# Layer 1's embedding products moved from the first layer's last attention head to the point between the last gate product and the latent attention

## The chip, the cores and the metric

The kernel runs on one core of one Trainium2 chip. The metric is the device time of one execution in microseconds (us), the median of several runs. Before the change it is 1482.28 us, the median of three runs from 1481.83 to 1483.80.

## What is computed

A decoder trunk of two layers on 1024 tokens of width 1024, in float32. Cut to what matters here:

```
def reference(x, p, ...):
    h = x
    for i in range(2):
        hn = rmsnorm(h, norm_g[i])
        m = even_layer(hn, ...) if i % 2 == 0 else odd_layer(hn, ...)
        h = h + m
        h = h + sigmoid(h @ ple_w_gate[i]) * (p[i] @ ple_w_proj[i])
    return h

def odd_layer(h, ...):
    z = h @ w_in
    cq, ckv, k_rope, c_gate, qkv, d_b, d_a, d_gate = split(z)
    # latent attention, 4 heads of 128: causal softmax(q k^T / sqrt(192)) v, gated by silu(c_gate)
    # gated delta rule, 4 heads of 128, chunks: one triangular solve a chunk, then a scan; gated by silu(d_gate)
    return concatenate([oc, od]) @ w_out
```

The even layer (layer 0) has a pooling mixer and six heads of differential attention. The products `p[i] @ ple_w_proj[i]`, 1024 x 256 by 256 x 1024, are the "embedding products": they depend on the inputs alone, and may be done at any time before the last step of their layer.

## The kernel before

**Products.** Each float32 operand is split into a rounded high part and the rest (`split`: a cast on ScalarE, line 134, and a difference on VectorE, line 135), and each product is three matmuls, high x high, high x low and low x high (lines 142 to 144). A bank of 128 x 512 results with a depth of 256 is thus six matmuls. One layer's embedding products are 8 output blocks (j in two groups of four) x 2 halves of the tokens = 16 banks = 96 matmuls.

**Order.** The program is written as Python generators that are stepped side by side; a list scheduler then sets each engine's order, and each engine runs its list strictly in that order. Accumulator banks in PSUM are shared: two called `acc`, two `s`, one `tr`, one `o`, two `x`. Loads and stores are nearly all issued by SyncE (SP) in one list; a store that has to wait for its data holds back all that stands behind it in that list.

**Layer 0's last part.** Heads 0 to 4 of the differential attention have the next head's projection beside them as filling work. Head 5 has no next head, so `ple_both()` fills it: the embedding products of layer 0 and of layer 1, one after the other. The results are copied from PSUM to tiles `z` (ScalarE line 127, VectorE line 129, in turn) and stored to `ple` in HBM. What of it is not used up beside head 5 is done after it. Then `out_stage` multiplies the mixer's output by `w_out`.

**Layer 1's middle.** After the projections come two products for the gates (`gate_proj`, here `gp1` is the second one, token tiles t0 to t7, 24 matmuls each; lines 907 to 909). Beside it stand the last preparation of the delta rule (`gdn_prep`), `block_solve` (the inverse of all 32 x 32 triangular blocks, 62 VectorE instructions that follow each from the one before, lines 990 and 992, whose result `xinv` goes to HBM and comes back as `U`), and `mla_prep` of head 0: for each half of the tokens it loads `zk`, `zq` and `V`, and transposes 4 x 4 blocks (line 1138) into one `acc` bank at a time, from which ScalarE (line 1139) and VectorE (line 1140) make the high and low parts of K and Q. The tags `zq` have two buffers, one for zk and one for zq, so the second half can be loaded only when the first half's transposes have read theirs. After this the latent attention (`mla_attn`: scores lines 1155 to 1159, softmax line 257, transposes line 275, values line 268) runs beside the delta rule (`gdn_solve`, from line 1000; `gdn_half`).

```
block_solve(nt)
istack.close()
istack, mp = open_pool("mla")
...
ahead = mla_prep(0, st)
step(ahead, gp1, gp1, ahead, ahead, gp1, gp1, ahead, gp1)
```

The functions that the change touches:

Of the kernel before, what the change touches and what calls it, by code (L numbers as in the profile page):

```python
# [56 lines left out]
def trunk_kernel(ctx, tc, a, out, layers=2):  # L57
# [520 lines left out]
        finish(1)  # L578
        yield

    def ple_both():

        for layer in range(layers):
            slots = [xt() for _ in range(8)]
            pT = [[None, None] for _ in range(2)]
            for h in range(2):
                for k in range(2):
                    hi, lo = slots[4 * h + 2 * k], slots[4 * h + 2 * k + 1]
                    split(hi, lo, stage(a["pT"][layer, k * P:(k + 1) * P, h * 512:(h + 1) * 512]))
                    pT[k][h] = (hi, lo)  # L590
            for gq in range(2):
                if gq == 0:
                    yield
                w = wload(a["ple_w_proj"][layer], 512 * gq, 512, nk=2)
                for j in range(4):
                    t = T("z", 2, (2, 512))
                    for h in range(2):
                        ps = bank("acc")
                        proj_T(pT, w, j, h, ps)
                        copy(h, t[:, h], ps)  # L600
                        dma.dma_start(ple[layer][4 * gq + j][h], t[:, h])
                    yield

    def fresh():
        return dict(Q=[], K=[], V=[], G=[])
# [13 lines left out]
    for hd in range(6):  # L619
        at, late = even_attn(hd, st), ahead  # L620
        if hd < 5:
            st = fresh()
            ahead = even_proj(hd + 1, st)
        else:
            ahead = ple_both()
        step(at, at, ahead, late, done, at, at, ahead, at, at, ahead, at, ahead, at, at)
        done = at
    step(done)
# [491 lines left out]
            s.activation(ct, tr, AF.Identity, scale=onorm)  # L1120
            dma.dma_start(cat[1][4 + hd][h], ct)

    def mla_prep(hd, st):
        for h in range(2):
            zq, zk = T("zq", 2, (4, 256), pool=mp), T("zq", 2, (4, 256), pool=mp)

            Q, K, V = T("Q", 3, (3, 512), F32R, mp), T("K", 3, (4, 512), F32R, mp), T("V", 4, pool=mp)
            for n, t in (("Q", Q), ("K", K), ("V", V)):
                st[n].append(t)
            dma.dma_start(zk, qkv[h][:, :, hd, 256:512])  # L1130
            dma.dma_start(zq, qkv[h][:, :, hd, 0:256])
            dma.dma_start(c3(V), qkv[h][:, :, hd, 512:640])
            yield
            for z, lo, dst, hb, lb, part in ((zk, 0, K, 2, 3, slice(0, P)), (zk, P, K, 0, 1, slice(0, P)),
                                             (zq, 0, Q, 1, 2, slice(0, P)), (zq, P, Q, 0, 0, slice(64, P))):
                ps = bank("acc")
                for c in range(4):
                    pe.transpose(ps[:, c * P:(c + 1) * P], z[:, c, lo:lo + P], ident)  # L1138
                s.copy(dst[:, hb, :], ps)
                v.tensor_tensor(out=dst[part, lb, :], in0=ps[part], in1=dst[part, hb, :].bitcast(F32), op=ALU.subtract)  # L1140
            yield
# [73 lines left out]
            step(cv, prep, cv, prep, cv, prep, prep)  # L1215
            prep = gdn_prep(hd, h, *outs)
    step(gp1, prep, gp1, prep, gp1, prep, prep)
    block_solve(nt)
    istack.close()
    istack, mp = open_pool("mla")  # L1220
    PW[0], PBUFS[1] = T_, 1
    PBUFS[0] = 2
    st = dict(Q=[], K=[], V=[])
    ahead = mla_prep(0, st)
    step(ahead, gp1, gp1, ahead, ahead, gp1, gp1, ahead, gp1)
    bstack.close()
    xstack.close()
    sstack, pools["scan"] = open_pool("scan", "right")
    astack, pools["y"] = open_pool("attn")

    def gdn():
        parts = [(pair, h, {}) for pair in ((0, 1), (2, 3)) for h in range(2)]
# [7 lines left out]
        sstack.close()  # L1240

    rec = gdn()
    for hd in range(H):
        at = mla_attn(hd, st)
        st = dict(Q=[], K=[], V=[])
# [80 lines left out]
```

## Time and profile before

| | |
|---|---|
| median of three runs | 1482.28 us |
| profiled execution | 1483.52 us |
| its span, first to last instruction | 1481.8 us |
| mean granted TensorE clock | 0.990 of full speed |
| TensorE (PE) busy | 1420.4 us, 96% of the span |
| VectorE (DVE) busy | 988.9 us, 67% |
| ScalarE (ACT) busy | 662.1 us, 45% |
| GpSimd (POOL) busy | 212.6 us, 14% |
| HBM read and written | 161 MB, 109 GB/s over the span |

The profile is of one execution. "Idle before" in its rows is the time that an engine stood still before an instruction, with the instruction of another engine that ended the wait. PEld is the loading of weights into TensorE, beside its matmuls. The granted clock has two levels, 2.4 GHz (1.0) and 1.2 GHz (0.5); a window's value between them is a mean over it. Matmuls are pipelined, so their durations overlap: what a matmul takes in a stream is the distance between two starts. An engine's busy share is a mean over stages with different limits.

### The profile page before, as it was taken

Reading aid. Unit: us, or ns where it says so; the run is one execution under the profiler, and the core shown is the slowest. Engines: PE = TensorE matmul, PEld = TensorE weight load, DVE = VectorE, ACT = ScalarE, POOL = GpSimd, SP = SyncE. Lnnn points to the kernel's source line nnn. Section 1 sums busy time; section 2 is a strip of 40 time slices with the busy share of each in tenths; the row PEclk is TensorE's granted clock in tenths of the full one; section 3 lists DMA queues with packets and bytes.
Section 4 is the critical chain, followed back from the end, with each engine's and each line's share of the span. In section 5 each row is a group of like instructions: output and inputs, shape, how many; then the busy total and the mean of one; then the engine's idle time right before and its main releaser. Section 6 shows DMA issues by size and latency. Waiting matters only on the chain. (4 is left out here: it accounts for less than half of the span.)

```text
span 1481.8 us, 22778 instructions
## 1 busy us (share of the span) xinstructions
PE 1420.4 (96%) x7495; PEld 1157.4 (78%) x7495; DVE 988.9 (67%) x2926; ACT 662.1 (45%) x1652; POOL 212.6 (14%) x347
## 2 busy tenths in 40 slices
PE   8899999999998999999998999999889999999998
PEld 6677888888887778888886777888768888877886
DVE  8645767676676857356668789988577888643342
ACT  6325656565656742134445434443223446722220
POOL 6230101011111001012104441110000000000021
PEclk9899999999999999999999999999989999999999
DMA  6215323232335582344424343233455634343432
GB/s 215 61 49 131 86 72 99 59 107 51 100 94 156 157 275 76 95 132 144 119 49 141 152 148 116 94 122 130 141 178 177 219 120 148 122 149 100 128 107 85
DMA packets 127749, 181.52 MB, mean 123 GB/s; under 512 B 28536, under 2 KB 55440, under 8 KB 127632
## 3 DMA queue, kind: packets, MB, share of 16 engines
q1 hardware_dynamic: 127632, 180.08, 39.8%
q8 instruction: 59, 0.97, 0.3%
q14 instruction: 58, 0.48, 0.1%
HBM read 108.20 MB, written 52.95 MB: 109 GB/s over the span
## 5 line engine op out<-in xcount | busy, mean ns | idle before, releaser
L142 PE MATMUL acc<-wh,x 128*128 128x512 f32 (+1 forms) x576 | 230.6, 401 | 0.6 <-DVE g L465 0.4
L143 PE MATMUL acc<-wl,x 128*128 128x512 f32 (+1 forms) x576 | 228.9, 397 | 1.7 <-DVE wl L135 1.7
L144 PE MATMUL acc<-wh,x 128*128 128x512 f32 (+1 forms) x576 | 227.3, 395 | 0.0
L142 PE MATMUL acc<-x,wh 128*128 128x512 f32 x536 | 215.8, 403 | 4.5 <-ACT wh L134 3.2
L144 PE MATMUL acc<-x,wl 128*128 128x512 f32 x536 | 214.0, 400 | 4.0 <-DVE wl L135 4.0
L143 PE MATMUL acc<-x,wh 128*128 128x512 f32 x536 | 212.5, 397 | 0.0
L134 ACT CAST wh<-raw 128x512 fp32r<-128x512 f32 (+2 forms) x184 | 106.8, 600 | 81.2 <-PE acc L143 37.5
L135 DVE TENSOR_TENSOR wl<-raw,wh 128x512 fp32r<-128x512 f32 (+2 forms) x184 | 120.7, 674 | 28.9 <-ACT wh L134 27.2
L143 PEld LDWEIGHTS acc<-wl,x 128*128 128x128 f32 x576 | 108.7, 189 | 25.3 <-DVE wl L135 2.8
L142 PEld LDWEIGHTS acc<-wh,x 128*128 128x128 f32 x576 | 108.5, 189 | 24.2 <-PE acc L144 0.8
L144 PEld LDWEIGHTS acc<-wh,x 128*128 128x128 f32 x576 | 108.5, 188 | 22.5
L144 PEld LDWEIGHTS acc<-x,wl 128*128 128x128 f32 x536 | 101.3, 189 | 30.4 <-DVE wl L135 7.1
L142 PEld LDWEIGHTS acc<-x,wh 128*128 128x128 f32 x536 | 101.0, 189 | 29.5 <-ACT wh L134 4.0
L143 PEld LDWEIGHTS acc<-x,wh 128*128 128x128 f32 x536 | 101.2, 189 | 22.4 <-issue 0.2
L680 POOL TENSOR_TENSOR u<-hp,hp 128x512 f32<-128x512 f32 x32 | 44.3, 1385 | 486.9 <-DVE hp L135 206.6
L261 ACT ACTIVATE p<-p,mx 128x128 f32<-128x128 f32 (+7 forms) x128 | 99.4, 777 | 32.9 <-DVE mx L257 24.1
L143 PE MATMUL acc<-hp,wh 128*128 128x512 f32 x256 | 101.6, 397 | 0.0
L142 PE MATMUL acc<-hp,wh 128*128 128x512 f32 x256 | 101.5, 396 | 0.0
L144 PE MATMUL acc<-hp,wl 128*128 128x512 f32 x256 | 101.5, 396 | 0.0
L257 DVE CUSTOM_DVE_ANT_0 p<-s,cst 128x512 f32<-128x512 f32 (+3 forms) x128 | 74.1, 585 | 29.4 <-PE s L534 15.4
L678 DVE SCALAR_TENSOR_TENSOR th<-th,ld 128x512 f32<-128x512 f32 x32 | 27.1, 848 | 77.2 <-ACT th L676 75.4
L461 ACT ACTIVATE z<-acc,rstd 128x256 f32<-128x256 f32 x48 | 22.8, 475 | 102.2 <-PE acc L144 99.4
(466 smaller groups left out, 2855.5 us busy)
## 6 DMA issues: line engine op xcount, KB each, us to landing
raw<-in_ev_w_in SPq DMA_DIRECT2D x56, 256.0 KB
Q<-sq SPq DMA_DIRECT2D x96, 128.0 KB
qkv<-zz SPq DMA_DIRECT2D x16, 640.0 KB
raw<-cat SPq DMA_DIRECT2D x32, 256.0 KB
ple<-z SPq DMA_DIRECT2D x32, 256.0 KB
raw<-in_ple_w_gate SPq DMA_DIRECT2D x32, 256.0 KB
ld<-ple SPq DMA_DIRECT2D x32, 256.0 KB
zq<-qkv SPq DMA_DIRECT2D x16, 512.0 KB
```

The source lines that it names most:

```text
L134: s.copy(hi, src)
L135: v.tensor_tensor(out=lo, in0=src, in1=hi.bitcast(F32), op=ALU.subtract)
L142: pe.matmul(ps, lh, rh, start=first, stop=False)
L143: pe.matmul(ps, lh, rl, start=False, stop=False)
L144: pe.matmul(ps, ll, rh, start=False, stop=last)
L257: v.tensor_tensor_reduce(out=pm[:, c * 512:c * 512 + n], in0=ps[:, 0:n], in1=mk, scale=-scale, scalar=prev, op0=ALU.add, op1=ALU.min, accu ...
L261: s.activation(pm[:, 0:w], pm[:, 0:w], AF.Exp, bias=prev, scale=-1.0, accum_out=sums)
L461: s.activation(z[:, t % 4, :], ps[:, 0:256], AF.Identity, scale=rstd[0][:, t:t + 1])
L678: v.scalar_tensor_tensor(out=th, in0=th, scalar=1.0, in1=r, op0=ALU.add, op1=ALU.mult)
L680: g.tensor_tensor(out=u, in0=hi.bitcast(F32), in1=lo.bitcast(F32), op=ALU.add)
```

## The change

`ple_both()` becomes `ple_proj(layer, slot, outs)`. Layer 0's embedding products stay beside head 5; each result is now a `z` tile of its own (two buffers, where two results shared a tile before). Layer 1's are started (loads and splits of `p`) in a new pool behind the opening of the pool `mla`; their 16 banks are stepped after the last gate tile and before the pool of the latent attention is opened. Their results go to the tiles `raw` (four buffers), the tag of the weights' loads, all copied by ScalarE. `block_solve` is written behind the opening of the pool and behind the first step of the embedding products. The first `mla_prep` takes its banks in turn from `s` and `x` (two each) in place of `acc`, and is stepped in turn with the gate tiles in another pattern.

```diff
-    def ple_both():
...
+    def ple_proj(layer, slot, outs):
+
+        pT = [[None, None] for _ in range(2)]
+        for h in range(2):
+            for k in range(2):
+                hi, lo = slot(), slot()
+                split(hi, lo, stage(a["pT"][layer, k * P:(k + 1) * P, h * 512:(h + 1) * 512]))
+                pT[k][h] = (hi, lo)
+        yield
+        for gq in range(2):
+            w = wload(a["ple_w_proj"][layer], 512 * gq, 512, nk=2)
+            for j in range(4):
+                for h in range(2):
+                    ps, t = bank("acc"), outs()
+                    proj_T(pT, w, j, h, ps)
+                    copy(h * (1 - layer), t, ps)
+                    dma.dma_start(ple[layer][4 * gq + j][h], t)
+                yield
...
-            ahead = ple_both()
+            ahead = ple_proj(0, xt, lambda: T("z", 2, (2, 512))[:, 0])
...
-    def mla_prep(hd, st):
+    def mla_prep(hd, st, banks=("acc",)):
+        nb = 0
...
-                ps = bank("acc")
+                ps = bank(banks[nb % len(banks)])
+                nb += 1
...
-    block_solve(nt)
     istack.close()
     istack, mp = open_pool("mla")
+    fstack, fp = open_pool("embed")
+    fill = ple_proj(1, lambda: T("pT", 8, dt=F32R, pool=fp), lambda: wp.tile([P, 512], F32, tag="raw", bufs=4, name=nm("ple")))
+    step(fill)
+    block_solve(nt)
...
-    ahead = mla_prep(0, st)
-    step(ahead, gp1, gp1, ahead, ahead, gp1, gp1, ahead, gp1)
+    ahead = mla_prep(0, st, ("s", "x"))
+    step(ahead, gp1, gp1, ahead, gp1, ahead, gp1, ahead, gp1)
...
-    astack, pools["y"] = open_pool("attn")
...
     rec = gdn()
+    step(*[fill] * 8)
+    fstack.close()
+    astack, pools["y"] = open_pool("attn")
```

Where instructions stand before and after, at three places. First TensorE's list at the end of head 5 before the change (`tr` are the last transposes of head 5, `acc1602` the last bank of layer 0's embedding products, `acc1622` the first bank of layer 1's):

```order
L143 MATMUL acc1602_6013<-x1422_5426,wh1589_5941 128x512
L564 MATMUL tr1580_5907<-cst_66,o1476_5584 128x128 x2
L144 MATMUL acc1602_6013<-x1421_5425,wl1590_5942 128x512
L564 MATMUL tr1580_5907<-cst_66,o1476_5584 128x128 x2
L142 MATMUL acc1622_6059<-x1603_6022,wh1616_6047 128x512
L143 MATMUL acc1622_6059<-x1604_6023,wh1616_6047 128x512
```

and the same place after the change (`acc1609` is the last bank of layer 0's embedding products, `acc1659` the first bank of `out_stage`):

```order
L564 MATMUL tr1583_5910<-cst_66,o1477_5585 128x128 x4
L142 MATMUL acc1609_6020<-x1421_5431,wh1590_5939 128x512
L143 MATMUL acc1609_6020<-x1422_5432,wh1590_5939 128x512
L144 MATMUL acc1609_6020<-x1421_5431,wl1591_5940 128x512
L142 MATMUL acc1609_6020<-x1424_5437,wh1593_5945 128x512
L143 MATMUL acc1609_6020<-x1425_5438,wh1593_5945 128x512
L144 MATMUL acc1609_6020<-x1424_5437,wl1594_5946 128x512
L142 MATMUL acc1659_6133<-x1611_6037,wh1636_6086 128x512
```

The 96 matmuls of layer 1's embedding products no longer stand between head 5 and `out_stage`. Two more banks of layer 0's stand behind the last values of head 5 than before.

Second, TensorE's list in layer 1's middle before the change, at the end of gate tile t4 (`acc2733`); `zq` are the loaded q and k tiles of head 0, the first four rows of L1138 their first half's transposes, L1155 and L1156 the first scores, and `acc2744` gate tile t5, behind which t6 and the second half's transposes follow:

```order
L144 MATMUL acc2733_11591<-wh2690_11294,x1994_7780 128x512
L1138 MATMUL acc2735_11620<-cst_66,zq2727_11555 128x128 x4
L1138 MATMUL acc2736_11627<-cst_66,zq2727_11555 128x128 x4
L1138 MATMUL acc2737_11634<-cst_66,zq2726_11554 128x128 x4
L1138 MATMUL acc2738_11641<-cst_66,zq2726_11554 128x128 x4
L1155 MATMUL s2757_11783<-K2729_11557,Q2728_11556 128x128
L1156 MATMUL s2757_11783<-K2729_11557,Q2728_11556 128x128
L1155 MATMUL s2776_11880<-K2729_11557,Q2728_11556 128x256
L1156 MATMUL s2776_11880<-K2729_11557,Q2728_11556 128x256
L142 MATMUL acc2744_11656<-wh2669_11252,x1888_7261 128x512
```

and after the change (`acc2718` is gate tile t6, which follows t5 directly; L1136 are the same transposes; `acc2724` is t7):

```order
L144 MATMUL acc2718_11520<-wh2650_11102,x1954_7588 128x512
L1136 MATMUL s2707_11455<-cst_66,zq2699_11390 128x128 x4
L1136 MATMUL x2708_11462<-cst_66,zq2699_11390 128x128 x4
L1136 MATMUL s2709_11469<-cst_66,zq2698_11389 128x128 x4
L1136 MATMUL x2710_11476<-cst_66,zq2698_11389 128x128 x4
L1136 MATMUL s2720_11549<-cst_66,zq2714_11513 128x128 x4
L1136 MATMUL x2721_11556<-cst_66,zq2714_11513 128x128 x4
L142 MATMUL acc2724_11577<-wh2629_11060,x1848_7069 128x512
L143 MATMUL acc2724_11577<-wl2630_11061,x1848_7069 128x512
```

Both halves' transposes now stand one behind the other between t6 and t7. Behind t7 the 96 matmuls of the embedding products follow, with the first two tiles of scores between their halves.

Third, VectorE's list at the end of `block_solve` before the change (`nx` is the inverse, L257 the first softmax, L1016 the transposes of `U`, which comes back from `xinv`):

```order
L990 TENSOR_TENSOR tm_11484<-nx_11483,nx_9531 128x31
L992 TENSOR_TENSOR nx_11483<-nx_11483,tm_11484 128x31
L908 SCALAR_TENSOR_TENSOR gz_11767<-gz_11767,acc_11742 128x512
L257 ISA p_11782,mx_11789<-s_11783,cst 128x128
L257 ISA mx_11789 128x1
L257 ISA p_11879,mx_11886<-s_11880,cst 128x256
```

and after the change (L986 and L988 are the solve, `wl` the low parts of the second half of the embedding weights, L1012 to L1014 the transposes of `U`):

```order
L986 TENSOR_TENSOR tm_11323<-nx_11322,nx_9339 128x31
L988 TENSOR_TENSOR nx_11322<-nx_11322,tm_11323 128x31
L135 TENSOR_TENSOR wl_11705<-raw_11703,wh_11704 128x512
L135 TENSOR_TENSOR wl_11711<-raw_11709,wh_11710 128x512
L1012 STREAM_TRANSPOSE wk_11828<-U_11817 32x32 x4
L1013 STREAM_TRANSPOSE wk_11828<-U_11817 32x32 x4
L1014 STREAM_TRANSPOSE wk_11828<-U_11817 32x32 x4
L1012 STREAM_TRANSPOSE wk_11932<-U_11921 32x32 x3
L257 ISA p_11802,mx_11809<-s_11803,cst 128x128
```

The first softmax now stands behind the transposes of `U`, and so behind the way of `xinv` to HBM and back.

And SP's list after the change, at the same place (`ple` are the stores of the embedding results, each of which waits for its copy, `U` the loads of the inverse):

```order
L158 DMA raw_11703<-in_ple_w_proj 128x512
L597 DMA ple_3_1_122<-ple_11694 128x512
L158 DMA raw_11709<-in_ple_w_proj 128x512
L989 DMA xinv<-nx_11322 128x1024
L999 DMA L_11920<-gL_0_7661 128x512
L1004 DMA vb_11928<-gvb_0_7653 128x512
L1005 DMA kw_11929<-gkw_0_7637 128x512
L1002 DMA U_11817<-xinv 32x4x32
L597 DMA ple_4_0_123<-ple_11716 128x512
L597 DMA ple_4_1_124<-ple_11726 128x512
L1002 DMA U_11817<-xinv 32x4x32
L597 DMA ple_5_0_125<-ple_11736 128x512
```

The loads of the second half of the embedding weights, the store of `xinv` and the four loads of the first `U` stand among the stores; the fourth load of `U` stands behind the fifth of the second half's eight stores.

## Rows read from the trace of the kernel before

**Rows 1.** The page's first part: busy time, share of the span, instructions.

```profile
PE 1420.4 (96%) x7495; PEld 1157.4 (78%) x7495; DVE 988.9 (67%) x2926; ACT 662.1 (45%) x1652; POOL 212.6 (14%) x347
```

**Rows 2.** Timeline of TensorE, end of head 5 (start, duration, count [idle before]).

```profile
525.03 0.48 PE L142 MATMUL acc<-x,wh 128*128 128x512 f32 x1
...
526.05 0.39 PE L143 MATMUL acc<-x,wh 128*128 128x512 f32 x1
526.28 0.40 PE L144 MATMUL acc<-x,wl 128*128 128x512 f32 x1
...
548.64 0.50 PE L142 MATMUL acc<-x,wh 128*128 128x512 f32 x1
```

**Rows 3.** Groups by line, 524 to 550 us: ScalarE's copies of embedding results.

```profile
L127 ACT COPY z<-acc 128x512 f32<-128x512 f32 x8 | 4.7, 587 | 8.6 <-DMA ple<-z 5.8 <-PE acc L144 2.6
```

**Rows 4.** Timeline of TensorE beside head 5.

```profile
479.23 1.97 PE L493 MATMUL x<-cst,z 128*128 128x128 f32 x8 [2.68 <-POOL z L242]
```

**Rows 5.** Windows: length, busy PE, PEld, DVE, ACT, POOL; PEclk, DMA, GB/s.

```profile
1060.00:1070.00 10.00, 5.72 (x28) 4.29 (x26) 4.67 (x16) 1.75 (x3) 0.00 (x0) 0.97 0.70 214
1070.00:1080.00 10.00, 9.50 (x36) 7.79 (x37) 9.14 (x22) 1.17 (x2) 0.00 (x0) 0.69 0.51 155
1080.00:1090.00 10.00, 8.88 (x48) 6.96 (x46) 8.42 (x20) 3.03 (x5) 0.00 (x0) 1.00 0.19 55
1090.00:1100.00 10.00, 7.17 (x30) 4.97 (x28) 6.80 (x22) 1.77 (x4) 1.49 (x4) 1.00 0.60 188
1100.00:1110.00 10.00, 7.36 (x60) 5.21 (x60) 5.65 (x28) 2.58 (x8) 0.00 (x0) 0.66 0.92 279
1110.00:1340.00 230.00, 223.25 (x1766) 191.42 (x1767) 163.35 (x617) 110.93 (x236) 7.94 (x14) 1.00 0.50 155
```

**Rows 6.** Timeline of TensorE in layer 1's middle.

```profile
1066.12 0.66 PE L1138 MATMUL acc<-cst,zq 128*128 128x128 f32 x4 [1.06 <-DVE gz L908]
1070.50 1.97 PE L1138 MATMUL acc<-cst,zq 128*128 128x128 f32 x8 [3.72 <-DVE K L1140]
...
1073.31 0.63 PE L142 MATMUL acc<-wh,x 128*128 128x512 f32 x1
1073.73 0.63 PE L143 MATMUL acc<-wl,x 128*128 128x512 f32 x1
...
1098.01 0.44 PE L1155 MATMUL s<-K,Q 128*128 128x384 f32 x1 [1.71 <-DVE mx L257]
...
1102.64 0.80 PE L268 MATMUL o<-V,pt 128*128 128x128 f32 x2 [3.43 <-DVE r L1163]
```

**Rows 7.** The same windows at 1 us: clock and DMA traffic.

```profile
1070.00:1071.00 1.00, 0.50 (x3) 0.50 (x4) 1.00 (x3) 0.00 (x0) 0.00 (x0) 0.50 1.09 355
1071.00:1072.00 1.00, 1.00 (x6) 0.87 (x5) 0.91 (x3) 0.35 (x1) 0.00 (x0) 0.50 0.41 126
1098.00:1099.00 1.00, 0.90 (x4) 0.55 (x4) 0.00 (x0) 0.48 (x2) 0.00 (x0) 1.00 0.99 383
```

**Rows 8.** Timeline of SP: issues of loads and stores.

```profile
1066.81 0.53 SPq L1130 DMA_DIRECT2D zq<-qkv  x1
...
1096.69 0.33 SPq L993 DMA_DIRECT2D xinv<-nx  x1
...
1099.42 0.32 SPq L1006 DMA_DIRECT2D U<-xinv  x1
```

**Rows 9.** Timeline of VectorE: block_solve's first and last, first softmax, U.

```profile
1065.98 0.18 DVE L990 TENSOR_TENSOR tm<-nx,nx 128x31 f32<-128x31 f32 x1
...
1096.42 0.21 DVE L992 TENSOR_TENSOR nx<-nx,tm 128x31 f32<-128x31 f32 x1
...
1097.66 0.28 DVE L257 CUSTOM_DVE_ANT_0 p<-s,cst 128x128 f32<-128x128 f32 x1
...
1102.75 0.48 DVE L1016 STREAM_TRANSPOSE wk<-U 32x32 f32<-32x32 f32 x4
```

**Rows 10.** Page's fifth part: splits' low part on VectorE.

```profile
L135 DVE TENSOR_TENSOR wl<-raw,wh 128x512 fp32r<-128x512 f32 (+2 forms) x184 | 120.7, 674 | 28.9 <-ACT wh L134 27.2
```

More of the change, by code (lines that the diff above doesn't have):

```diff
@@ L579, in even_attn @@
         yield
-    def ple_both():
[L583 to L597, printed above, removed]
-                        ps = bank("acc")
[L599 to L602, printed above, removed]
+    def ple_proj(layer, slot, outs):
[15 more added lines that the diff above has]
+                yield
     def fresh():
@@ L1135, in mla_prep @@
                                              (zq, 0, Q, 1, 2, slice(0, P)), (zq, P, Q, 0, 0, slice(64, P))):
-                ps = bank("acc")
+                ps = bank(banks[nb % len(banks)])
+                nb += 1
                 for c in range(4):
```

## The prediction

> **What bounds the kernel now.** I read the page's busy times first: TensorE works 1420.4 of 1481.8 us [rows 1], so a change can win only what TensorE loses in idle stretches or at the lower clock, or what it does needlessly. The work itself stays the same here: every product, transpose and solve is there before and after. So the question is in which of its holes TensorE will stand afterwards. The timeline of TensorE answers that in two stretches.
>
> The first is the end of head 5. Layer 1's embedding products follow head 5's last transposes without a wait from 525.03 to 548.64 us, 23.6 us for 96 matmuls; the starts inside are 0.233 us apart [rows 2]. They fill no hole there; they are pure TensorE time ahead of `out_stage`.
>
> The second is layer 1's middle. In the windows from 1060 to 1110 us TensorE is busy for 5.72, 9.50, 8.88, 7.17 and 7.36 of 10 us, 38.6 of 50 together, and in two of them the mean granted clock is 0.69 and 0.66 [rows 5]. From 1110 to 1340 us it is busy 223 of 230 at full clock: there is nothing to fill later. So idle time in this middle is 50 - 38.6 = 11.4 us, most of it in four waits: 1.06 and 3.72 us between the first transposes, 1.71 for the softmax of the first scores, 3.43 for the first softmax's sum [rows 6]. The clock costs on top of it. After the 3.72 us of idleness the matmuls start 0.42 us apart [rows 6], the clock is at its lower level, 1.2 GHz [rows 7]; a mean of 0.69 over the window from 1070 is 6.2 us at half speed, of which TensorE worked 5.6: 2.8 lost. After the 3.43 us it is the same from 1102.6 to about 1106.5, some 2 lost (0.66 in that window, a part of it idle).  Holes before, in us of full-speed TensorE: 11.4 + 2.8 + 2.1 = 16.3.
>
> **What the move takes away.** At the end of head 5 the 96 matmuls go. If nothing else moved, `out_stage` would start 23.6 us earlier. Two things take from that. Two more banks of layer 0's embedding products (12 matmuls, 12 x 0.233 = 2.8 us) stand behind head 5's last values than before, and the values end when head 5's softmax chain lets them, not when the products do. And beside head 5 the wait of 2.68 us for GpSimd [rows 4] has one group of transposes and fewer products ahead of it than before. Also each result now has a `z` buffer of its own, two in all, while before two results shared one of two, four in all; ScalarE's copies already waited 5.8 us for stores in this stretch [rows 3]. Halved buffering may hold up the last banks by as much as that, or by nothing since only a few banks are left back to back. I take 23.6 - 2.8 - 0.5 = 20.3 us gained, with ends at 23.6 (the two banks stand in a hole) and 17.5 (another 2.8 lost to the wait for GpSimd and the copies).
>
> **What it puts in, in the middle.** 96 matmuls at 0.233 us are 22.4 us; their 16 copies on ScalarE (0.59 us each [rows 3], 9.4 us) lie beside them, one for every 1.4 us of TensorE. Now the holes. Without the transposes between t4 and t5, t5 and t6 (48 matmuls, 11.2 us) run on from 1064.46 to 1075.7, and the first half's transposes, in four banks, no longer wait for one another: the 1.06 and 3.72 us go, and the lower clock behind them. They end at about 1077. But the second half's transposes now stand right behind, and the tags `zq` have two buffers, so `zk` of the second half is loaded only after the first half's zk transposes have read it, at about 1076.4. In the trace that load was issued at 1066.81 [rows 8]; it and a load behind it, 0.77 MB, move until 1071.4 at about 355 GB/s [rows 7], so its own 512 KB took some 3.8 us. Hence 1080.2, and a wait of **3.2 us** in the place of 3.72. As 3.72 us of idleness brought the lower clock, I count its 2.8 us once more. t7 then ends at about 1080.2 + 5.6 + 1.6 for the transposes + 2.8 = 1090.2.
>
> The first half of the products takes 11.2 us, to 1101.4, the first two tiles' scores 1.3. The second half's weights come late. Their loads stand in SP's list behind the stores of the seventh and the eighth result, and these tiles and the weights share the four buffers of `raw`. So the loads issue only at about 1101 and 1102.5. Nothing in the trace shows this load in this place; with the 3.8 us of zk as an upper end and the 2.73 us from the store of xinv to the first load of `U` [rows 8] as a lower one, they land from 1104 to 1106, and cast and low part (0.59 and 0.67 us [rows 3, 10]) come on top. That is a hole of **3.4 us** (between 1 and 5, and up to 2.8 more if the clock falls again). Holes after: 3.2 + 2.8 + 3.4 = 9.4.
>
> `block_solve` runs on VectorE from 1065.98 to 1096.42 with K's and Q's low parts in between [rows 9]. It starts as before, but the first low part of K stands after its 13th instruction and waits for the transposes behind t6: VectorE stands for some 6 us, and the embedding weights' low parts (0.67 us each) join. So it ends at about 1104, not 1096.4. Behind it stands xinv's way out and back, 6.3 us from 1096.42 to the first transpose of `U` at 1102.75 [rows 9]. The first softmax, before at 1097.66 [rows 9], now stands behind these transposes, at 1111 to 1117. The second half of the products covers TensorE until 1105.5 + 11.2 = 1116.7: the cover is just long enough. From there on the stretch is dense as before.
>
> **The sum.** The middle comes out later against its start by 22.4 + 9.4 - 16.3 = 15.5 us; the end of head 5 gives 20.3. Net 15.5 - 20.3 = -4.8 us. The profiled execution took 1483.5 and the median is 1482.3, so the forecast is 1478.7 against the one and **1477.5** for the median.
>
> **A rule against it.** The row first: after 3.72 us of idleness the clock was at its lower level, and after the 1.71 us before 1098.01 it was not (1.00 in the window of 1098) [rows 6, 7]. The Trainium skill ("TensorE: Matmul & The Clock Gate", part 1) says that the throttled clock is the default and that only activity releases it, so that each wait is paid again after it ends. By that, the third wait would bring 2.8 us more, and the sum would be -2.0 instead of -4.8; by the row of 1.71 us alone it would not. This trace shows the clock falling after the long waits and not after the short ones, and a wait of 3.4 us is nearer to the long ones; it stands in the range.
>
> **Rivals.**
> *Larger gain.* The holes are small: the second half's zk comes before its transposes are reached, the weights' loads are issued early. Then about 2.9 us of holes are left, the middle costs 22.4 + 2.9 - 16.3 = 9.0, the end of head 5 gives the full 23.6: -14.6, **1467.7**. For it: before, transposes of the same kind followed with waits of 0.2 to 0.5 us once the data lay there. Against: two buffers for `zq`.
> *No change.* All three waits take their upper ends, with the clock: holes of 3.2 + 2.8 + 5 + 2.8 = 13.8, the middle costs 19.9: **1482**. For it: SP's list, and DMA traffic of 279 GB/s over the window from 1100 with 383 at its height [rows 5, 7], to which 4 MB of stores come (16 x 256 KB), now in that stretch.
> *Slower.* The solve becomes the bound. The loads of `U` stand between the stores of the second half's results; a store that waits for its copy holds `U` back, and behind `U` stand the transposes, and behind them the first softmax. If the last needed `U` goes out only behind the last copies (1116.7 + 0.6), it lands 2.7 us later at 1120; the transposes take 1.5, the softmax to the first values 5 (1097.66 to 1102.64): 1126.5 against 1102.64, 23.9 later, less 2.7 of scores done ahead: 21.2. With 17.5 gained at head 5 that is +3.7, **1486**. It decides from the point where the middle is later by more than the 17.5 to 20.3 gained. For it: the first softmax's new place in VectorE's list. Against: four loads of `U` are enough for the first transposes, and the fourth stands behind the fifth of eight stores only.
> In a sentence by itself: the Trainium skill ("DMA: Bandwidth & Descriptors", on the anatomy of one DMA) says that waits happen on the issuing sequencer before dispatch, which is this mechanism, and that one transfer has a fixed cost of about 2.0 us; by its figures the first `U` load would land 2.0 us after its issue, and the slower case would be 1485. No row shows a `U` load held by a store.
>
> **Chances.** Forecast 0.42, larger gain 0.24, no change 0.20, slower 0.14. A measurement of this kernel can tell 0.2%, 3 us, from no change. The forecast's own range is 1473 to 1481; the part of it within the bound and the part of the no-change case below it are about equal, so faster is 0.66, same 0.20, slower 0.14. The range for 8 in 10 leaves out the far ends: 1467.5 to 1484.
>
> **What would show it.** Right: `out_stage` begins near 528 us; no idleness between t4 and t6, one wait of about 3 us before the second half's transposes with the lower clock after it; a second wait before the second half of the products; first softmax between 1091 and 1097 on the new clock (the old less 20). Wrong: `out_stage` begins after 532, TensorE waits for head 5's copies, a wait stands behind the products for the first softmax, or the attention after it loses its 97% density.

## The result and the profile after

The changed kernel takes 1478.91 us (median of 18 runs, 1476.07 to 1481.43), the kernel before 1485.93 in the same comparison (18 runs, 1481.83 to 1492.26). The ratio is 0.9945, with a 95% interval from 0.9932 to 0.9959: faster by 0.55%, some 8 us by the ratio and 7.0 by the medians. Forecast were 1477.5 us, faster, against a median of 1482.3 from three runs. The two profiled executions lie closer together, 1483.52 and 1479.85, 3.7 us apart; why that is less than the medians' 7.0 is settled further down. In the experiments below, two runs of the banks alone (1709 and 2782 us) and two of the kernel before (2775 and 3530) are left out of the ratios.

The first part of the page after answers to [rows 1]: the same 7495 matmuls, TensorE's busy time within 1.4 us of before, in a span that is 3.9 us shorter (1477.9).

```profile
PE 1419.0 (96%) x7495; PEld 1158.4 (78%) x7495; DVE 985.1 (67%) x2918; ACT 666.2 (45%) x1660; POOL 207.0 (14%) x347
```

The end of head 5, in TensorE's timeline after (start, duration, count, idle before in brackets), answers to [rows 2, 4]:

```profile
477.43 0.33 PE L493 MATMUL x<-cst,z 128*128 128x128 f32 x1 [1.72 <-POOL z L242]
...
525.09 1.02 PE L564 MATMUL tr<-cst,o 128*128 128x128 f32 x4 [1.01 <-DVE o L557]
526.07 0.50 PE L142 MATMUL acc<-x,wh 128*128 128x512 f32 x1
...
527.58 0.40 PE L142 MATMUL acc<-x,wh 128*128 128x512 f32 x1
```

Behind head 5's transposes stands one bank of layer 0's products (526.07), and at 527.58 `out_stage` begins, before at 548.64. The wait for GpSimd has become shorter, 1.72 instead of 2.68 us, and the lower clock that stood behind it before (0.50 from 479 to 482 us, some 1.5 us lost) is gone.

Layer 1's middle, in TensorE's timeline after, answers to [rows 6]:

```profile
1062.90 1.08 PE L1136 MATMUL s<-cst,zq 128*128 128x128 f32 x4 [3.11 <-DMA zq<-qkv]
...
1071.65 0.39 PE L142 MATMUL acc<-pT,wh 128*128 128x512 f32 x1
...
1083.25 0.22 PE L1154 MATMUL s<-K,Q 128*128 128x128 f32 x1
...
1088.68 0.80 PE L142 MATMUL acc<-pT,wh 128*128 128x512 f32 x1 [4.23 <-ACT wh L134]
...
1094.22 0.50 PE L142 MATMUL acc<-pT,wh 128*128 128x512 f32 x1 [0.49 <-ACT ple L127]
```

The transposes now go to the banks `s` and `x` and no longer wait for one another. One wait of 3.11 us is left, for `zk` of the second half. The first half of the products runs from 1071.65, the first two tiles' scores (all but one matmul of them) from 1083.25, and then TensorE stands 4.23 us for the second half's weights.

The windows after (length, busy PE, PEld, DVE, ACT, POOL, granted clock, DMA share, GB/s) answer to [rows 5]; the work ahead of the middle stands 17.8 us earlier than there:

```profile
1060.00:1070.00 10.00, 7.10 (x33) 6.16 (x34) 9.39 (x21) 5.34 (x10) 1.03 (x3) 0.83 0.88 281
1070.00:1080.00 10.00, 9.96 (x44) 7.85 (x43) 9.32 (x23) 3.62 (x6) 0.00 (x0) 1.00 0.88 289
1080.00:1090.00 10.00, 5.77 (x27) 4.74 (x26) 6.79 (x22) 3.00 (x5) 0.00 (x0) 0.81 0.97 304
1090.00:1100.00 10.00, 9.51 (x35) 7.22 (x35) 2.04 (x13) 2.83 (x5) 0.00 (x0) 0.84 0.51 184
...
1110.00:1340.00 230.00, 225.37 (x1757) 192.25 (x1757) 165.58 (x608) 113.88 (x241) 7.61 (x13) 1.00 0.50 156
```

The two holes show at 7.10 and 5.77 of 10 busy, the lower clock behind them at 0.83, 0.81 and 0.84. From 1110 us on it is denser than before, 225.37 of 230 against 223.25.

Why the second half's weights come late, and why the first softmax does, stands in SP's list of issues after, which answers to [rows 8]:

```profile
1083.70 0.33 SPq L158 DMA_DIRECT2D raw<-in_ple_w_proj  x1
1084.13 0.42 SPq L597 DMA_DIRECT2D ple<-ple  x1
1084.64 0.45 SPq L158 DMA_DIRECT2D raw<-in_ple_w_proj  x1
1086.72 0.32 SPq L989 DMA_DIRECT2D xinv<-nx  x1
...
1091.00 0.32 SPq L1002 DMA_DIRECT2D U<-xinv  x1
1094.20 0.81 SPq L597 DMA_DIRECT2D ple<-ple  x2
1095.06 0.45 SPq L1002 DMA_DIRECT2D U<-xinv  x1
```

The loads of `raw` alternate with the stores of `ple`, and between the first and a later load of `U` two more stores wait for their copies. VectorE's timeline after, against [rows 9]: the solve's last row, a transpose of `U`, the first softmax.

```profile
1086.44 0.21 DVE L988 TENSOR_TENSOR nx<-nx,tm 128x31 f32<-128x31 f32 x1
...
1093.34 0.48 DVE L1012 STREAM_TRANSPOSE wk<-U 32x32 f32<-32x32 f32 x4 [2.74 <-DMA U<-xinv]
...
1102.26 0.29 DVE L257 CUSTOM_DVE_ANT_0 p<-s,cst 128x128 f32<-128x128 f32 x1
```

The first softmax comes at 1102.26, later than the 1091 to 1097 forecast. TensorE doesn't feel it: its products last until about 1102.5.

**Where the time went.** Three marks in TensorE's timeline divide the profiled span: the start of layer 0's first scores (118.26 before, 119.35 after), the first `acc<-hp` matmul behind `out_stage` (638.34, 617.43), and layer 1's last `x<-cq,ck` matmuls (L959 before, L955 after; 1052.37, 1034.59), which end the work ahead of the middle. Net of the later start, the end of head 5 gives 20.9 + 1.1 = 22.0 us. Of these, 3.1 are lost again between the second mark and the third (17.8 + 1.1 = 18.9 left). From the third mark to layer 1's first output matmul it is 333.99 us before and 347.90 after: the middle costs 13.9. That leaves 18.9 - 13.9 = 5.0 us, and less the later start the 3.9 by which the span is shorter.

### The profile page after: what moved, and what is told of

It reads as the page before. It is cut to its first block, busy times and chain, and to the rows that moved or that the text cites. A ratio compares the mean times of both kernels' runs of the same rounds, so it can differ in the third digit from the quotient of the medians.

```text
span 1477.9 us, 22765 instructions
## 1 busy us (share of the span) xinstructions
PE 1419.0 (96%) x7495; PEld 1158.4 (78%) x7495; DVE 985.1 (67%) x2918; ACT 666.2 (45%) x1660; POOL 207.0 (14%) x347
## 4 chain that ended last, share of the span: by engine, by line
PE 70%; DVE 12%; ACT 7%; DMA 5%; issue 4%; POOL 1%; SPq 0%; DVEq 0%; ACTq 0%; POOLq 0%
PE acc L144 17%; PE acc L142 17%; PE acc L143 17%; PE o L268 4%; PE s L533 2%; PE tr L275 2%; DVE wl L135 1%; PE s L534 1%; DMA raw<-in_od_w_in 1%; ACT wh L134 1%; DVE p L257 1%; ACT sqj L917 1%; ACT p L261 1%; PE acc L1048 1%; DMA raw<-in_ev_w_in 1%
## 5 line engine op out<-in xcount | busy, mean ns | idle before, releaser
L144 PE MATMUL acc<-x,wl 128*128 128x512 f32 x504 | 201.9, 401 | 4.8 <-DVE wl L135 4.8
L142 PE MATMUL acc<-x,wh 128*128 128x512 f32 x504 | 203.6, 405 | 2.9 <-ACT wh L134 2.5
L143 PE MATMUL acc<-x,wh 128*128 128x512 f32 x504 | 200.7, 399 | 0.3 <-DVE x L138 0.3
L144 PEld LDWEIGHTS acc<-x,wl 128*128 128x128 f32 x504 | 95.6, 190 | 29.7 <-DVE wl L135 7.7
L142 PEld LDWEIGHTS acc<-x,wh 128*128 128x128 f32 x504 | 95.7, 190 | 26.1 <-ACT wh L134 3.5
L143 PEld LDWEIGHTS acc<-x,wh 128*128 128x128 f32 x504 | 95.6, 190 | 22.2 <-DVE x L138 0.7
L257 DVE CUSTOM_DVE_ANT_0 p<-s,cst 128x512 f32<-128x512 f32 (+3 forms) x128 | 74.2, 586 | 26.5 <-PE s L534 15.6
```

The lines of the kernel that those rows point to most:

```text
L142: pe.matmul(ps, lh, rh, start=first, stop=False)
L143: pe.matmul(ps, lh, rl, start=False, stop=False)
L144: pe.matmul(ps, ll, rh, start=False, stop=last)
L257: v.tensor_tensor_reduce(out=pm[:, c * 512:c * 512 + n], in0=ps[:, 0:n], in1=mk, scale=-scale, scalar=prev, op0=ALU.add, op1=ALU.min, accu ...
```

## The experiments

The account on trial is the prediction's ("Theory A" in the expectations): TensorE's own holes and its clock set the time of the middle, so that each of the two waits left is worth what it shows. The rivals: one of the two parts (four banks, or the moved products) does it all ("Theory B", for the banks); or VectorE with the solve, xinv and `U` is the bound, and TensorE's waits only show it ("Theory C"). Each ratio is against runs of the kernel before in the same comparison, on the same chip. That kernel's median was 1485.2, 1484.2 and 1487.4 us in the three comparisons, so ratios from different ones can differ by 0.2% through it alone. "Holes" are TensorE's idle time plus what the lower clock cost, added up over windows of 1 us of that stretch: 16.4 before (11.4 idle, 5.0 clock; 1050 to 1130 us), 11.6 after (7.95 and 3.6; 1034 to 1120).

**The banks alone.**

```
 kernel before, and:
-    ahead = mla_prep(0, st)
-    step(ahead, gp1, gp1, ahead, ahead, gp1, gp1, ahead, gp1)
+    ahead = mla_prep(0, st, ("s", "x"))
+    step(ahead, gp1, gp1, ahead, gp1, ahead, gp1, ahead, gp1)
```

> The kernel before with one part of the change alone: the first head's transposes in four banks and the new step order; the embedding products stay behind head 5. Theory A (the time comes from moving 22 us of products into holes of layer 1's middle): nothing fills the middle, the waits of 1.06 and 3.72 us go but a wait of about 3 us for the second half's zk comes, and the first softmax still has to stand behind block_solve, which now ends some us later; ratio to the kernel before 0.999 to 1.003. Theory B (the four banks and the step order make the gain): 0.994 to 0.996, as the whole change.

Measured: 1493.92 us, ratio 1.0048 [1.0024, 1.0073], slower, and by more than the account allowed. TensorE's timeline of this kernel:

```profile
1104.46 0.69 PE L1157 MATMUL s<-K,Q 128*128 128x384 f32 x1 [13.37 <-DVE mx L257]
```

and VectorE's:

```profile
1077.74 0.69 DVE L1142 TENSOR_TENSOR K<-s,K 128x512 fp32r<-128x512 f32 x1 [7.46 <-ACT K L1141]
```

Without the products behind the first scores, these wait 13.37 us for the first softmax: the solve ends 7.6 us later than before (its last row at 1103.99). K's and Q's low parts stood in the solve's list before as well, but there VectorE did not wait for the first of them; now their transposes stand behind t6, and VectorE stands 7.46 us for it. Holes of 29.8. The banks and the new step order make VectorE later, and only the moved products hide that.

**The move alone.**

```
 the changed kernel, and:
-    ahead = mla_prep(0, st, ("s", "x"))
-    step(ahead, gp1, gp1, ahead, gp1, ahead, gp1, ahead, gp1)
+    ahead = mla_prep(0, st)
+    step(ahead, gp1, gp1, ahead, ahead, gp1, gp1, ahead, gp1)
```

> The changed kernel with the old transposes (acc banks) and the old step order: the embedding products moved alone. Theory A: the waits of 1.06 and 3.72 us between the transposes and the lower clock behind them (2.8) are back, the 3.1 us for zk and its clock (1.4) are gone; so 2 to 5 us slower than the changed kernel, ratio to the kernel before 0.996 to 0.999. Theory B: no gain, 0.999 to 1.004. Theory C (the way of the inverse out and back to the first softmax bounds the middle): as the changed kernel, 0.9935 to 0.9955, since block_solve ends no later here.

Measured: 1486.46 us, ratio 1.0002 [0.9984, 1.0019]: no difference. Its TensorE timeline keeps the transposes' wait and gets the one for the weights as well:

```profile
1051.86 1.98 PE L1136 MATMUL acc<-cst,zq 128*128 128x128 f32 x8 [4.57 <-DVE K L1138]
...
1094.18 0.79 PE L142 MATMUL acc<-pT,wh 128*128 128x512 f32 x1 [4.21 <-ACT wh L134]
```

The end of head 5 gains as in the whole change, and the middle takes all of it (+23.5 us; holes of 19.2). So neither part gains alone, and together they give 0.9945.

**The first of the two waits left: the weights.** Both halves' weights are loaded ahead of the first products.

```
+        ws = {}
...
-            w = wload(a["ple_w_proj"][layer], 512 * gq, 512, nk=2)
+            for q in range(gq, 2 if layer else gq + 1):
+                if q not in ws:
+                    ws[q] = wload(a["ple_w_proj"][layer], 512 * q, 512, nk=2)
+            w = ws[gq]
```

> The changed kernel with both halves of the layer-1 embedding weights loaded ahead of the products, so that the second half's loads don't stand behind the stores. Theory A: the wait of 4.2 us between the halves and the lower clock behind it (about 2) go; the first softmax is then a little late: 3 to 6 us faster than the changed kernel, ratio to the kernel before 0.9905 to 0.9925. Theory C: TensorE waits as long for the first softmax, which the loads of U hold at about 1102: within 1 us of the changed kernel, 0.994 to 0.995.

Measured: 1474.69 us, ratio 0.9924 [0.9899, 0.9949]. The windows of this kernel, where the change had 5.77 of 10 and a clock of 0.81 and 0.84:

```profile
1080.00:1090.00 10.00, 10.00 (x44) 8.08 (x43) 5.21 (x18) 4.26 (x8) 0.00 (x0) 1.00 0.98 335
1090.00:1100.00 10.00, 9.91 (x64) 7.61 (x63) 4.88 (x28) 5.47 (x15) 0.00 (x0) 1.00 0.68 215
```

The wait is gone and nothing takes its place: holes of 6.4 instead of 11.6, and a middle of +9.9 instead of +13.9. It was TensorE's own wait, and worth most of what it shows: 4.0 us of the middle for 5.2 of holes.

**The second: `zk` of the second half.** The gate tile t7 is set ahead of the second half's transposes, so that it covers their load.

```
-    step(ahead, gp1, gp1, ahead, gp1, ahead, gp1, ahead, gp1)
+    step(ahead, gp1, gp1, gp1, gp1, ahead, ahead, gp1, ahead)
```

> The changed kernel with another step order: gate tiles t5 and t6 are stepped ahead of the first half's transposes and t7 ahead of the second half's, so that t7 fills the wait for the second half's zk. Theory A: the 3.1 us wait and the clock behind it (1.4) go: 3 to 5 us faster than the changed kernel, ratio to the kernel before 0.991 to 0.9925. Theory C: the products end earlier but the first softmax does not; within 1 us of the changed kernel, 0.994 to 0.995.

Measured: 1481.09 us, ratio 0.9964 [0.9948, 0.998], 2.2 us above the change by the medians (the two intervals overlap); the account missed, by which it had to be 3 to 5 us below. TensorE's timeline of this kernel:

```profile
1059.87 0.50 PE L142 MATMUL acc<-wh,x 128*128 128x512 f32 x1 [2.78 <-DVE gz L904]
...
1089.92 0.80 PE L142 MATMUL acc<-pT,wh 128*128 128x512 f32 x1 [6.63 <-ACT wh L134]
```

and SP's issues:

```profile
1083.36 0.32 SPq L989 DMA_DIRECT2D xinv<-nx  x1
1083.98 0.32 SPq L597 DMA_DIRECT2D ple<-ple  x1
1084.39 2.05 SPq L158 DMA_DIRECT2D raw<-in_ple_w_proj  x2
```

t7's bank isn't free: it waits 2.78 us for VectorE to read an earlier tile. And the weights now stand behind the store of xinv, so their wait grows from 4.23 to 6.63. The wait of 3.11 gave way to one of 2.78, and the one behind it grew by 2.4.

**Both edits.** 

> The changed kernel with the early weights of e3 and the step order of e4 together. In e4 the products' second half began no earlier, since the loads of its weights stand behind the store of xinv there, and so behind block_solve; with all weights loaded early that is gone. Theory A: 1 to 4 us faster than e3, ratio to the kernel before 0.990 to 0.992. Theory C (with the early weights the way of the inverse to the first softmax bounds): as e3, 0.992 to 0.993, with the first softmax again near 1094 us and TensorE idle or working on scores before it.

Measured: 1473.25 us, ratio 0.9923 [0.9904, 0.9941], as with the early weights alone. TensorE's timeline and a window of this kernel:

```profile
1059.80 0.50 PE L142 MATMUL acc<-wh,x 128*128 128x512 f32 x1 [2.78 <-DVE gz L908]
...
1073.61 0.50 PE L144 MATMUL acc<-pT,wl 128*128 128x512 f32 x1 [1.25 <-DVE wl L135]
```

```profile
1070.00:1080.00 10.00, 8.40 (x38) 6.41 (x38) 9.66 (x22) 4.19 (x8) 0.00 (x0) 1.00 0.96 308
```

VectorE is busy 9.66 of 10 us here, and TensorE's waits ahead of the products and at their start are for it: the wait for `zk` only moves.

**The stores off SP's list.** With the early weights, ScalarE issues layer 1's stores of `ple`, so that nothing stands ahead of the loads of `U`.

```
-                    dma.dma_start(ple[layer][4 * gq + j][h], t)
+                    (s if layer else dma).dma_start(ple[layer][4 * gq + j][h], t)
```

> e3 with the stores of layer 1's embedding results issued by ScalarE, which makes them, in place of SP: xinv and the loads of U no longer stand behind stores. Theory C: the first transposes of U come 2 to 4 us earlier than in e3 (1093.2), the solve behind them too; 1 to 3 us faster than e3, ratio to the kernel before 0.990 to 0.992. Theory A: the products end at 1093.6 as in e3, the first softmax is hidden behind them; as e3, 0.992 to 0.993. If issuing on ScalarE costs it time, its copies come late and it is slower.

Measured: 1484.25 us, ratio 0.9994 [0.9976, 1.0011]: the gain of the early weights is gone. SP's issues in this kernel, and VectorE's first transpose of `U`:

```profile
1086.41 0.32 SPq L993 DMA_DIRECT2D xinv<-nx  x1
...
1092.03 3.02 SPq L1006 DMA_DIRECT2D U<-xinv  x4
```

```profile
1096.10 0.48 DVE L1016 STREAM_TRANSPOSE wk<-U 32x32 f32<-32x32 f32 x4 [12.27 <-DMA U<-xinv]
```

The solve's last row is at 1083.61, but xinv is stored only at 1086.41 and `U` loaded at 1092.03: without the stores, 12 more loads than with the early weights alone stand ahead of the first load of `U` in SP's list. The stores had held those loads back. Behind the end of the products TensorE then stands for its first matmul on these transposes (the profile names no releaser), and the clock falls:

```profile
1096.40 0.28 PE L1023 MATMUL acc<-wk,L 32*32 32x32 f32 x2 [2.81 <-issue]
```

```profile
1100.00:1110.00 10.00, 10.00 (x61) 7.50 (x61) 6.10 (x27) 1.93 (x6) 0.30 (x1) 0.50 0.49 135
```

The clock stays at 0.50 until about 1112. Up to 1120 us this execution is idle 3.5 us longer than the one with the early weights alone and loses 6.6 more to the clock, so the larger part of its loss is the clock. With t7 ahead as well the time is the same:

> Early weights, t7 ahead and the stores on ScalarE together. If both theories are right in part (first TensorE's waits, then the inverse's way) this is the fastest: ratio to the kernel before 0.988 to 0.991. If the attention behind it can't use an earlier start, 0.992 to 0.993.

Measured: 1484.61 us, ratio 1.0001 [0.9983, 1.0019]; the first transposes of `U` only at 1099.06. The account missed here too. In the profiled execution the clock is at 1.00 behind the products and falls later, from about 1192 to 1202 us, which costs 5.1.

**Buffers of layer 0's results.** As before the change, two results share one `z` tile, four in flight instead of two.

```
-            ahead = ple_proj(0, xt, lambda: T("z", 2, (2, 512))[:, 0])
+            pair = []
+            def halves():
+                if not pair:
+                    t = T("z", 2, (2, 512))
+                    pair.extend((t[:, 0], t[:, 1]))
+                return pair.pop(0)
+            ahead = ple_proj(0, xt, halves)
```

> The changed kernel with two of layer 0's results sharing a z tile again (four in flight in place of two). The prediction counted 0.5 us for the halved buffering and 2.8 us for the two banks left behind head 5's last values. If that is so, out_stage begins 0 to 3 us earlier than in the changed kernel (net of the start of the run); if the copies never waited, within 0.3 us. Ratio to the kernel before 0.9925 to 0.995.

Measured: 1475.91 us, ratio 0.9942 [0.9922, 0.9963]: as the change by the ratio, 3.0 us below it by the medians of two comparisons. TensorE's timeline of this kernel at the end of head 5:

```profile
520.10 0.50 PE L142 MATMUL acc<-x,wh 128*128 128x512 f32 x1 [0.40 <-ACT z L127]
...
524.31 0.50 PE L564 MATMUL tr<-cst,o 128*128 128x128 f32 x2 [0.22 <-DVE o L557]
...
534.16 0.50 PE L142 MATMUL acc<-x,wh 128*128 128x512 f32 x1 [1.67 <-DVE t L663]
```

The row at 520.10 is `out_stage`'s first: it begins ahead of head 5's last transposes, and the wait for GpSimd near 476 us no longer shows. From the first scores it is 402.7 us to there, 408.2 in the change: 5.5 earlier. Off go 1.67 for the wait at 534.16 and 1.0 for the transposes that now lie inside `out_stage`; 2.8 are left, and the first `acc<-hp` matmul is earlier by just that (24.8 us against before, net of the start, instead of 22.0). The middle gives a part back (+15.9 instead of +13.9).

**The best of both.** Early weights with shared `z`, and then with t7 ahead too:

> e3 and e8 together: both halves of the weights loaded early, and layer 0's results two to a z tile again. e8 began out_stage 2.8 us earlier than the changed kernel, e3 closed the wait between the halves. If the two are independent: 1 to 3 us faster than e3, ratio to the kernel before 0.9895 to 0.992. If the earlier start is lost again in layer 1's middle (the loads there do not come earlier): as e3, 0.992 to 0.993.

Measured: 1471.86 us, ratio 0.9896 [0.9873, 0.9919], 2.8 us below the early weights alone, as expected if the two are independent.

> e5 and e8 together (early weights, t7 ahead, shared z tiles). As e9 if t7's place is of no account behind VectorE's list, which e5 against e3 suggests: ratio to the kernel before 0.9895 to 0.992, within 1.5 us of e9.

Measured: 1470.17 us, ratio 0.9879 [0.9856, 0.9903], the fastest version here and a little below what was expected; its interval overlaps the last one's. A window of it, for those of the change with 5.77 and 9.51:

```profile
1080.00:1090.00 10.00, 10.00 (x44) 8.03 (x44) 3.59 (x14) 4.10 (x7) 0.00 (x0) 1.00 0.89 312
1090.00:1100.00 10.00, 10.00 (x94) 7.63 (x93) 6.19 (x35) 4.60 (x12) 0.30 (x1) 1.00 0.59 183
```

**A shorter solve.** Both edits without shared `z`, and the solve cut from 31 steps to 13; it leaves out 36 of the solve's 62 VectorE instructions.

```
-        for j in range(31):
+        for j in range(13):
```

> e5 with block_solve cut from 31 steps to its first 13 (the rest of the inverse is left out, so 36 of its 62 VectorE instructions, some 14 us of VectorE time). Theory C, put more exactly: with TensorE's waits closed, VectorE's list (block_solve and the low parts, busy 9.4 of 10 us there) sets when t7's bank, the weights' low parts and the first softmax come. Then the first transposes of U come 6 to 14 us earlier, the products begin 0 to 3 us earlier, and the kernel is 2 to 6 us faster than e5, ratio to the kernel before 0.988 to 0.991. If TensorE's own work bounds the stretch now: within 1 us of e5, 0.992 to 0.993.

Measured: 1471.03 us, ratio 0.989 [0.9866, 0.9913], against 1473.25 for the same kernel with the whole solve, in another comparison (medians before 1487.4 and 1484.2). The first transposes of `U` come 16.9 us earlier (1075.32 instead of 1092.19), the first products no earlier, and the first softmax at 1093.94 instead of 1095.23, behind the products in both. So 16.9 us off the solve bring 2.2 by the medians. That lies in the range (2 to 6) that was expected with VectorE as the bound, and not within the 1 us expected with TensorE's own work as the bound; but of the two signs named for the former, an earlier `U` and earlier products, only the first came. What shows in TensorE's timeline is that its waits for VectorE's low parts around the start of the products, 0.69 and 1.25 us, shrink to one of 0.35, and that the products end 1.3 us earlier. VectorE's list still costs some us; most of the solve is hidden by the products. (`U` is another matter: its second transposes wait 12.64 us for loads in this run.)

**The kernel before once more**, unchanged, to see its spread.

> The kernel before once more, for a second profile of it: its runs spread from 1481 to 1492 us. If the spread comes from layer 1's middle, the stretch from the last gate tiles to layer 1's out_stage is longer here than the 334.0 us of the first profile by as much as the run is; if from the start or layer 0, that stretch is the same within 1 us. Ratio to the kernel before 0.998 to 1.002.

Measured: ratio 0.9991 [0.9965, 1.0017], as it should be; its profiled execution took 1489.88 us, the one ahead of the prediction 1483.52. Windows of 4 us of this run:

```profile
1102.00:1106.00 4.00, 3.62 (x13) 2.49 (x13) 2.58 (x15) 1.30 (x6) 0.00 (x0) 0.50 0.96 289
1106.00:1110.00 4.00, 4.00 (x24) 2.80 (x23) 2.17 (x9) 0.00 (x0) 0.00 (x0) 0.50 0.98 296
1110.00:1114.00 4.00, 4.00 (x34) 2.75 (x33) 1.51 (x7) 1.19 (x3) 0.00 (x0) 0.50 0.42 140
1114.00:1118.00 4.00, 4.00 (x23) 3.30 (x23) 1.79 (x7) 0.00 (x0) 0.30 (x1) 0.50 0.26 66
1118.00:1122.00 4.00, 4.00 (x28) 3.77 (x29) 1.26 (x12) 0.74 (x2) 0.13 (x1) 0.50 0.00 0
1122.00:1126.00 4.00, 4.00 (x59) 3.33 (x56) 2.42 (x11) 2.08 (x5) 0.40 (x1) 0.82 0.28 50
```

and of the execution that the prediction was made from:

```profile
1102.00:1106.00 4.00, 3.36 (x11) 2.48 (x11) 2.39 (x15) 1.51 (x6) 0.00 (x0) 0.50 0.97 285
1106.00:1110.00 4.00, 4.00 (x50) 2.73 (x49) 2.67 (x11) 0.91 (x3) 0.00 (x0) 0.89 0.96 290
```

Both have the wait for the first softmax's sum, 3.44 and 3.43 us, and the lower clock behind it. In one it is over by about 1107, in the other it lasts to about 1123: 2.1 us lost against 10.5. Up to that wait the two executions agree within 0.7 us. From the third mark to layer 1's first output matmul the one takes 334.0 us and the other 340.2, and the spans differ by 6.4 (1481.8 and 1488.1): the spread comes from the middle, by the expectation's own sign.

The mean granted clock of each run parts the kernel before in two. Of its 70 runs in the three comparisons and here, 38 show 0.989 or more and take at most 1486.65 us (median 1483.0), and 32 show 0.987 or less and take at least 1486.64 (median 1489.8).

**Parts without a run.** No run has `block_solve` alone back in its old place, and none has layer 1's results copied by VectorE in turn or kept out of `raw`; what these parts of the change do by themselves is not shown.

## Why the prediction was right, and where it was off

The sign, the size and the mechanism held: 7 us by the medians where 4.8 were forecast, inside the forecast's own range. That the profiled pair, net of the start, gives 5.0 us where the sum gave 4.8 is in part luck: 1.7 us too little at head 5 and 1.6 too much in the middle made up for 3.1 lost between them, which the sum did not have. The steps, one by one:

*End of head 5: right, low by 1.7.* 20.3 forecast, 22.0 measured. The 23.6 us were read as a stretch without a wait; they hold 1.2 of delays, among them 0.43 for a copy at 531.31, and the 96 matmuls alone are 22.4. From the first scores to the first `acc<-hp` matmul, TensorE's idle time and what the lower clock cost are 9.1 us before and 9.3 after, so the gain is these 22.4, and the terms taken off were named wrongly. The wait for GpSimd became shorter and lost the clock behind it; the halved `z` buffers, put at 0.5, cost 2.8 (6.6 us of holes with shared tiles). What the sum had not: 3.1 us of it are lost again by the third mark. TensorE is idle 1.8 us more there, above all at 715.10 (1.15 us) and 729.87 (1.79), where it waits for VectorE, and why stays open. Another 1.5 are the lower clock behind a wait of 1.52 us, which before has too (1.53 at 869.18) at full clock:

```profile
851.00:854.00 3.00, 2.87 (x7) 2.30 (x8) 2.46 (x11) 0.51 (x1) 1.48 (x3) 0.50 0.62 204
```

The runs of the move alone, the early weights, t7 ahead and both lose 2.8, 1.9, 1.2 and 1.8 us in this stretch; the first and the last of them show the lower clock there, the other two do not. So it need not belong to the change.

*The waits of the transposes: right.* 1.06 and 3.72 us are gone, and one of 3.11 stands in their place, forecast 3.2, with 1.4 us lost to the clock behind it where 2.8 were forecast.

*The weights: mechanism right, size low.* 3.4 us forecast, 4.23 + 0.49 measured, and the lower clock after it cost 2.2, where the sum had nothing and only the range had it. So the holes are 11.6, not 9.4. The row of 1.71 us without a slow clock [rows 6, 7] was the wrong neighbour. The Trainium skill ("TensorE: Matmul & The Clock Gate", part 1) says that the throttled clock is the default and that activity releases it. The trace agrees behind these two waits: the windows show 0.83 with the wait of 3.11 us, 0.81 and 0.84 with that of 4.23.

*The cost of the middle: too high.* 15.5 forecast, 13.9 measured, though the holes are bigger: 22.4 + 11.6 - 16.4 would be 17.6. Of the 3.7 between, 2.8 are idle time that the rest of the stretch lost, up to the first output matmul: 7.3 us before (from 1130 us on), 4.6 after (from 1120 on). The prediction took this part to be as dense as before. The last 0.9 is not located. Without this part the same account is 1.7 to 2.7 us too high for the banks alone, the move alone and the early weights.

*The softmax: too early.* 1091 to 1097 forecast, 1102.26 measured, though the solve ended close to where it was put (1086.44, for 1104 on the old clock). The mechanism of the slower rival, loads of `U` behind stores of `ple`, does act, though not on the first load: no such store stands between xinv (1086.72) and it (1091.00), and VectorE waits 2.74 us for it. For the later loads, each behind a store, it waits 3.18, 1.69 and 2.16. The Trainium skill ("DMA: Bandwidth & Descriptors", on the anatomy of one DMA) says that such waits lie on the issuing sequencer; SP's rows at 1094.20 and 1095.06 agree. The fixed cost of 2.0 us that the prediction took from that section stands there for transfers that GpSimd issues; here SP issues the first load of `U` at 1091.00, and VectorE reads it 2.3 us later. The mechanism did not decide, since the products cover TensorE to the same point. That cover is tight; the banks alone, which have no products there, show a wait of 13.37 us.

*The base: one term mis-sized.* "Some 2" for the clock behind the 3.43 us wait was read from an execution in which it was short. In another it is 10.5, and this one place makes nearly all of the difference between those two executions. The change takes that wait away, so it gains 3.7 us against the first and more against the others, 7.0 over the medians (3.7, and 2.4 by which before's profiled run lies below its median, and 0.9 by which the other lies above). The runs fit: before spreads over 10.4 us, the change over 5.4. The base of the forecast, 1482.3 from three runs, belongs to the shorter half of before's runs: of the 18, the nine shorter have a median of 1483.8, and the change's median lies 4.9 below that, where 4.8 were forecast; the nine longer have 1489.9, and 11.0. So the 7.0 stands between the two. That all of the longer runs have their lower clock in this one place is inferred: their mean clock is lower, but only two executions of before were seen in a trace.

## To carry to other kernels

Work that is moved to fill a hole and the edit that shapes the hole are to be priced together: here each alone gave nothing or a loss, and both gave 0.55%. What a queue's list holds back is part of its order: before a store is taken off it, look at what moves up. And before one execution is taken for the kernel, look at its spread: a stretch at the lower clock behind one wait can make most of it.

## What the runs showed of the hardware

The lower clock, once there, can outlast the wait by far while TensorE works without pause: at 0.50 in the windows of the kernel before run once more from 1106 to 1122 us, 4.00 of 4 busy in each that is shown, where the same program behind the same wait was back at full clock by about 1107 in another execution. With the stores on ScalarE's list it was 0.50 from 1100 to 1110 behind a wait of 2.81 us, 10.00 of 10 busy. The rule named above, by which activity releases the clock, fits the second of these three executions better than the other two; what made the difference does not show in the rows.
